# Gate and up products of a hybrid decoder layer: 512-column matmuls over the high and low part together, joins on VectorE, and a first weight sum accumulated by DMA

## The chip, the cores and the metric

The kernel runs on one core of one Trainium2 chip. The metric is device time in microseconds for one execution. The kernel before takes 619.7 us (median of 3 runs, 619.35 to 620.3). The engines spoken of are PE (TensorE matmuls; PEld is its weight load), DVE (VectorE), ACT (ScalarE), POOL (GpSimd, which here mostly issues DMAs) and SP (SyncE, which issues the plain loads). Each engine works off its own queue strictly in the order in which the program emits instructions.

## The reference

One decoder layer on 512 tokens of width 1024: an input projection, retention and sparse attention heads, an output projection with layer norm, and then the part that is changed here, the gated FFN:

```python
x = layer_norm(DEEPNORM_ALPHA * x + mix, ln_mix_gain, ln_mix_bias)
gate, up = jnp.split(x @ w_gate_up, 2, axis=-1)      # 1024 -> 2 x 2816
ffn = (jax.nn.silu(gate) * up) @ w_down              # 2816 -> 1024
return layer_norm(DEEPNORM_ALPHA * x + ffn, ln_ffn_gain, ln_ffn_bias)
```

## The kernel before

All is fp32. PE multiplies in a rounded form (`fp32r`), so every operand is split into a high part (rounded) and a low part (the rest), and a product is three matmuls: high by high, low by high, high by low. The helper `split` (L85 to L91) makes the parts: ACT copies the source into the rounded type (L86); the low part is either a subtraction on DVE (L91), or, when its engine is `None`, a negated copy on ACT (L88) to which a DMA issued by POOL adds the source (L89).

The FFN's first product is staged in 22 *cycles* (`g_cycle(n)`, L883, n = 0 to 21), one for each 128 hidden columns of gate and up. Tokens are cut into two halves of 256, the inner dimension into two halves of 512, and gate and up are the two halves of the columns; a scheme of Winograd's kind forms the 2 x 2 block product with seven block products in place of eight. The block operands of x are made ahead (`parts["11"]`, `["12"]`, `["22"]` and four sums `["s1"]` to `["s4"]`, each 128 x 2 (high, low) x 4 x 256). Those of the weights come from one raw load of 1 MB (`graw[n]`, gate `g` and up `u`; three buffers, loaded by SP) and four sums on DVE (`g_sum`, L824): `gs0` to `gs3`. In the text the four pieces that `g_conv` splits are called **A** (two 512-column halves, `gs1` and `gs0`), **B** (gate, raw), **C** (`gs2` and `gs3`) and **D** (one half, up, raw). A, B and C take their buffers `wh` and `wl` from a ring of four, and so does D.

In cycle n PE runs seven *steps* (`g_mm`, L849, 12 matmuls of 256 columns each), here named by their weight piece, with a prime where they belong to n + 1:

A0 into bank `ga(n)`; A1 into `gc(n)`; B0' into `ga(n+1)`; C0 into `ga(n)`; B1' into `gb(n+1)`; C1 into `ga(n)`; D into `gc(n)`.

Banks are read between the steps that add to them: ACT copies `ga` after A0 (`t2`, L894), after C0 (`t7`, L916) and after B0' (`t1`, L863); DVE adds `gc` to `t7` (L925) before D adds to `gc`; DVE adds `gb` (L867), ACT applies Silu to it (L871), and ACT applies Silu to the second token half straight from `ga` after C1 (L952). `g_end` (L877) adds `gc` to `t2` and multiplies both halves in the next cycle. So C0 may not start before ACT has read `ga` for t2, C1 not before it has read it for t7, and D not before DVE has read `gc`. The hidden units land in `hu`, six tiles of four slots; the sixth is in memory slot `s9`.

Beside step C1 and D, the cycle makes the weights of the next: B of n + 2, the sums of n + 2, C and D of n + 1; A of n + 1 is made in the middle of cycle n. The raw load of n + 4 is issued at the end of cycle n and waits until raw buffer n + 1 is no longer read. `FIRST = 4` is the first cycle whose B steps run inside another cycle. In cycle 21 nothing is left to make for gate and up, and `prepare_down` (L1247) converts the first weights and hidden units of the down projection in its place (`conv_w`, `conv_h`).

Of the kernel before, what the change touches and what calls it, by code (L numbers as in the profile page):

```python
# [53 lines left out]
def hybrid_layer_kernel(ctx: ExitStack, tc: tile.TileContext, xT, x, pos, w0, wf, wt, wo,  # L54
# [760 lines left out]

    def g_sum(n, eng=V, which=slice(0, 4)):
        if n >= NF:
            return
# [4 lines left out]
        for dst, a, b in ((0, u[:, :S], g[:, :S]), (1, u[:, S:], t[0]), (2, u[:, S:], u[:, :S]), (3, g[:, S:], t[1]))[which]:
            eng.tensor_tensor(t[dst], a, b, op=ALU.subtract)  # L824
# [23 lines left out]

    def g_mm(n, acc, kind, i, q, first):  # L849
        h, l = gw[n, kind]  # L850
        steps = [(k, a, b) for k in range(4) for a, b in ((h, 0), (l, 0), (h, 1))]
        if n == 0:
            steps.sort(key=lambda x: x[2])
        for j, (k, a, b) in enumerate(steps):
            T.matmul(gp[n][acc], lhsT=a[:, i * S + k * P:i * S + k * P + P], rhs=parts[q][:, b, k],  # L855
                     start=first and j == 0, stop=j == 11, skip_group_check=True)
# [4 lines left out]

    def g_t1(n):
        A.copy(gp[n]["h1"], gp[n]["a"])  # L863

    def g_add1(n):
        h1 = gp[n]["h1"]
        V.tensor_tensor(h1, h1, gp[n]["b"], op=ALU.add)  # L867
# [9 lines left out]
    def g_end(n):  # L877
        g = gp[n]
        V.tensor_tensor(g["t2"], g["t2"], g["c"], op=ALU.add)
        V.tensor_tensor(g["h1"], g["h1"], g["t2"], op=ALU.mult)  # L880
        V.tensor_tensor(g["h2"], g["h2"], g["t7"], op=ALU.mult)

    def g_cycle(n, between=None):  # L883
# [10 lines left out]
        A.copy(gp[n]["t2"], gp[n]["a"])  # L894
# [16 lines left out]
        c = gp[n]["c"]  # L911
        if n == NF - 1:
            c = tmp("gc")[:, :Q]
            A.copy(c, gp[n]["c"])
# [596 lines left out]
```

## Time and profile before

| what | before |
|---|---|
| median of 3 runs | 619.7 us |
| the profiled execution | 619.74 us |
| its span in the profile | 617.9 us |
| of the span: gate and up, from the first `ga` to the first `dl` matmul | 273.4 to 498.2 us |
| ACT, share of the span busy | 52% |
| DMA bytes | 97.97 MB |

The profiled execution's span lies 1.8 us below its own time; the rest is outside what the profile records. Engine times in a timeline are a start and a length; matmuls overlap, so their pace is read from start to start. "idle before" says what an engine waited for.

### The profile page before, as it was taken

How to read it: one execution, taken by the hardware profiler on the slowest of the kernel's cores; microseconds unless marked ns; L12 is line 12 of the kernel's file. 1: busy time of each engine (PE TensorE's matmuls, PEld its weight loads, DVE VectorE, ACT ScalarE, POOL GpSimd, SP SyncE). 2: the span in 40 equal slices, each digit the busy share in tenths (PEclk: the TensorE clock that was granted, in tenths of full speed). 3: DMA queues.
4: the chain of work that ended last, by engine and by line, in shares of the span. 5: the costliest groups of instructions: out<-in, count | busy, mean ns of one | idle time of the engine just before them, and what ended most of it. 6: DMA issues, size and time to landing. Idle time of an engine off the chain costs nothing.

```text
span 617.9 us, 9846 instructions
## 1 busy us (share of the span) xinstructions
PE 608.2 (98%) x3732; PEld 545.6 (88%) x3732; DVE 512.8 (83%) x953; ACT 323.0 (52%) x576; POOL 114.0 (18%) x118
## 2 busy tenths in 40 slices
PE   9999999999999999999999999999999999999994
PEld 7988888888888878889999999999999988888884
DVE  6897687898879877979998989898888888977856
ACT  5643444334343765777754555555455685648300
POOL 1176232421455000242000000000000021214010
PEclk9999999999999999999999999999999999999998
DMA  9887444778533962596333232332323379589602
GB/s 307 290 227 207 132 112 126 185 177 218 136 103 102 322 266 94 134 232 131 91 132 137 74 133 85 121 100 106 118 88 124 102 192 221 157 226 300 195 35 102
DMA packets 31584, 97.97 MB, mean 159 GB/s; under 512 B 3328, under 2 KB 9024, under 8 KB 25904
## 3 DMA queue, kind: packets, MB, share of 16 engines
q1 hardware_dynamic: 20464, 76.23, 35.9%
q0 software_dynamic: 10336, 19.86, 17.9%
q10 hardware_dynamic: 736, 1.25, 0.6%
q8 instruction: 29, 0.48, 0.3%
q14 instruction: 19, 0.16, 0.1%
HBM read 74.52 MB, written 2.10 MB: 124 GB/s over the span
## 4 chain that ended last, share of the span: by engine, by line
PE 82%; DVE 6%; issue 5%; DMA 3%; POOL 2%; ACT 1%; POOLq 0%; DVEq 0%; ACTq 0%
PE ga L855 19%; PE gc L855 10%; PE pf L95 5%; PE pf L94 5%; PE pf L96 5%; PE gb L855 4%; PE acc L205 4%; PE dl L95 2%; PE dl L96 2%; PE dl L94 2%; PE pt L94 2%; PE pt L96 2%; PE pt L95 2%; PE dr L96 2%; PE dr L95 2%
## 5 line engine op out<-in xcount | busy, mean ns | idle before, releaser
L86 ACT CAST wh<-raw 128x1024 fp32r<-128x1024 f32 x43 | 45.0, 1050 | 50.9 <-issue 20.6
L89 POOL DMA_DIRECT2D slot<-hu x9 | 10.9, 1337 | 235.0 <-ACT slot L88 233.8
L94 PE MATMUL pf<-xh,wh 128*128 128x512 f32 x128 | 50.0, 391 | 0.0
L95 PE MATMUL pf<-xl,wh 128*128 128x512 f32 x128 | 50.0, 390 | 0.0
L96 PE MATMUL pf<-xh,wl 128*128 128x512 f32 x128 | 49.9, 390 | 0.0
L91 DVE TENSOR_TENSOR wl<-raw,wh 128x1024 fp32r<-128x1024 f32 x24 | 29.1, 1224 | 14.2 <-ACT wh L86 14.2
L94 PE MATMUL pt<-wh,xh 128*128 128x512 f32 x96 | 39.1, 408 | 0.0
L96 PE MATMUL pt<-wh,xl 128*128 128x512 f32 x96 | 37.6, 391 | 0.0
L95 PE MATMUL pt<-wl,xh 128*128 128x512 f32 x96 | 37.5, 390 | 0.0
L824 DVE TENSOR_TENSOR gs<-graw,gs 128x512 f32<-128x512 f32 x44 | 30.3, 689 | 0.8
L440 POOL TENSOR_TENSOR rs<-ve,half 128x1 f32<-128x1 f32 (+1 forms) x11 | 11.8, 1069 | 102.6 <-DVE ve L439 102.4
L824 DVE TENSOR_TENSOR gs<-graw 128x512 f32<-128x512 f32 x44 | 30.2, 685 | 0.0
L96 PEld LDWEIGHTS pf<-xh,wl 128*128 128x128 f32 x128 | 24.0, 188 | 5.1
L94 PEld LDWEIGHTS pf<-xh,wh 128*128 128x128 f32 x128 | 24.0, 188 | 4.6
L95 PEld LDWEIGHTS pf<-xl,wh 128*128 128x128 f32 x128 | 24.1, 188 | 4.5
L89 POOL DMA_DIRECT2D wl<-raw x19 | 16.9, 891 | 59.2 <-ACT wl L88 52.3
L402 DVE MAX8 m<-score 128x8 f32<-128x256 f32 (+2 forms) x48 | 26.8, 558 | 1.1
L403 DVE MATCH_REPLACE8 score<-m,score 128x256 f32<-128x256 f32 (+2 forms) x48 | 26.0, 543 | 0.0
L385 ACT ACTIVATE lg<-lg 128x256 f32<-128x256 f32 (+2 forms) x24 | 10.9, 474 | 24.6 <-PE lg L384 22.6
L96 PEld LDWEIGHTS pt<-wh,xl 128*128 128x128 f32 x96 | 18.0, 188 | 3.9
L95 PEld LDWEIGHTS pt<-wl,xh 128*128 128x128 f32 x96 | 18.1, 189 | 3.1
L94 PEld LDWEIGHTS pt<-wh,xh 128*128 128x128 f32 x96 | 18.1, 188 | 3.1
(1123 smaller groups left out, 2076.3 us busy)
## 6 DMA issues: line engine op xcount, KB each, us to landing
graw<-in_wgu_dram SPq DMA_DIRECT2D x22, 1024.0 KB, 4.8
wl<-raw POOLq DMA_DIRECT2D x19, 512.0 KB, 5.6
raw<-in_wf_dram SPq DMA_DIRECT2D x8, 1024.0 KB, 7.4
raw<-in_wo_dram SPq DMA_DIRECT2D x8, 1024.0 KB, 4.8
raw<-in_wt_dram SPq DMA_DIRECT2D x6, 1024.0 KB, 5.5
r<-in_wd_dram SPq DMA_DIRECT2D x12, 512.0 KB, 5.6
draw<-in_wd_dram SPq DMA_DIRECT2D x8, 512.0 KB, 5.8
w0s<-in_w_dram SPq DMA_DIRECT2D x8, 320.0 KB, 4.8
```

Source lines behind the costliest of these rows:

```text
L86: A.copy(hi, src)
L89: nc.gpsimd.dma_start(lo.bitcast(F32), src, accum_op=ALU.add)
L91: eng_lo.tensor_tensor(lo, src, hi.bitcast(F32), op=ALU.subtract)
L94: T.matmul(acc, lhsT=lh, rhs=rh, start=first, stop=False, **kw)
L95: T.matmul(acc, lhsT=lh, rhs=rl, start=False, stop=False, **kw)
L96: T.matmul(acc, lhsT=ll, rhs=rh, start=False, stop=last, **kw)
L205: T.matmul(acc0[i][:, o:], lhsT=a[:, i * P:i * P + P], rhs=b[kt][:, o:], start=(kt == 0 and p == 0), stop=(kt == KT - 1 and p == 2))
L402: V.max(m8, a)
L403: V.match_replace(out=a, in_to_replace=m8, in_values=a, imm_value=TAKEN)
L440: G.tensor_tensor(r[:, :n], e[:, :n], half[:, :n], op=ALU.pow)
L824: eng.tensor_tensor(t[dst], a, b, op=ALU.subtract)
L855: T.matmul(gp[n][acc], lhsT=a[:, i * S + k * P:i * S + k * P + P], rhs=parts[q][:, b, k], start=first and j == 0, stop=j == 11, skip_group ...
```

## The change

From n = 4 on (`wide(n)`), three things are different; cycles 0 to 3 keep their form.

* A step is 8 matmuls. Four have 512 columns: the high weights against the high and the low part of x side by side, into a whole bank, whose first half then holds high by high and whose second half high by low. Four have 256 columns: the low weights against the high part, into the first half. The two halves of a bank are added on DVE (`g_join`) after the copy or the sum has been made 512 wide.
* Sum `gs0` is made in its own place in memory slot `s9` (`firsts`): SP loads half of up there ahead (`g_ahead`), and POOL issues a DMA that adds half of gate straight from memory (`g_plus1`). Sum `gs2` is made in the raw buffer by a DMA of the same kind (`g_plus3`). Signs are turned so that the sums are additions; the minus goes to the copies `t2` and `t7` (`g_minus`) and to the subtractions after them. DVE is left with two of the four sums. The first combinations of x (`combine`) are written with another operation for the same reason.
* The low part of D always goes by ACT and an adding DMA, up to n = 14 into a tile of its own in `s10` (`lasts`). The order within a cycle is another: for n + 1 below 15, A is made ahead of t2 and B and D ahead of t7; from there on (`late`), A stands behind t2, B behind the join of t7, and D at the cycle's end.

```diff
     def g_sum(n, eng=V, which=slice(0, 4)):
...
+        if n >= FIRST:
+            t = gsum[n] = [firsts(n), tmp(f"gs{n}_1"), u[:, :S], tmp(f"gs{n}_3")]
+            eng.tensor_tensor(t[1], u[:, S:], t[0], op=ALU.add)
+            eng.tensor_tensor(t[3], g[:, S:], t[1], op=ALU.add)
+            return
...
+    def g_ahead(n):
+        if FIRST <= n < NF:
+            dma(firsts(n), wgu[order[n], :, 1, :S])
+    def g_plus1(n):
+        if FIRST <= n < NF:
+            nc.gpsimd.dma_start(firsts(n), wgu[order[n], :, 0, :S], accum_op=ALU.add)
+    def g_plus3(n):
+        if FIRST <= n < NF:
+            u = graw[n][:, 1]
+            nc.gpsimd.dma_start(u[:, :S], u[:, S:], accum_op=ALU.add)
...
     def g_conv(n, kind, eng=V, into=None):
...
+        if kind == "D" and wide(n):
+            eng = None
...
     def g_mm(n, acc, kind, i, q, first):
         h, l = gw[n, kind]
+        if wide(n):
+            ws = [slice(i * S + k * P, i * S + k * P + P) for k in range(4)]
+            for k in range(4):
+                T.matmul(two(gp[n][acc]), lhsT=h[:, ws[k]], rhs=parts[q][:, :, k], start=first and k == 0, stop=False,
+                         skip_group_check=True)
+            for k in range(4):
+                T.matmul(gp[n][acc][:, :Q], lhsT=l[:, ws[k]], rhs=parts[q][:, 0, k], start=False, stop=k == 3,
+                         skip_group_check=True)
+            return
...
+    def g_join(t):
+        V.tensor_tensor(t[:, :Q], t[:, :Q], t[:, Q:], op=ALU.add)
...
     def g_cycle(n, between=None):
...
+        if wide(n) and not late:
+            g_conv(n + 1, "A")
...
+        g_minus(n, "t2", "a")
...
+        if n == 0 or wide(n) and late:
+            g_conv(n + 1, "A")
...
+        if wide(n):
+            g_sum(n + 2)
+            if not late:
+                g_conv(n + 2, "B")
         g_mm(n, "a", "C", 0, "s3", False)
...
+        if wide(n):
+            if not late:
+                g_conv(n + 1, "D")
+                g_plus1(n + 4)
+            g_seven(n)()
+            g_join(gp[n]["t7"])
+            if between:
+                next(between)
+            if late:
+                g_conv(n + 2, "B")
+            g_mm(n, "a", "C", 1, "22", False)
+            if nxt:
+                g_add1(nxt)
+            g_conv(n + 1, "C")
+            if nxt:
+                g_silu1(nxt)
+            if n < NF - 1:
+                g_mm(n, "c", "D", 0, "s4", False)
+            A.copy(gp[n]["h2"], gp[n]["a"][:, Q:])
+            V.tensor_tensor(gp[n]["h2"], gp[n]["h2"], gp[n]["a"][:, :Q], op=ALU.add)
+            A.activation(gp[n]["h2"], gp[n]["h2"], AF.Silu)
+            if late:
+                g_conv(n + 1, "D")
+                g_plus1(n + 4)
+            g_plus3(n + 3)
+            g_load(n + 4)
+            g_ahead(n + 5)
+            return
```

First place: ACT around the end of cycle 3, before the change. `gh4C` and `gh5A` are the high parts of C of 4 and A of 5, `hu` Silu results, `gt` is t2 of 4.

```order
L871 ACTIVATE hu_3103<-hu_3103 128x256
L86 CAST gh4C<-gs_2_3048 128x512
L86 CAST gh4C<-gs_3_3049 128x512
L952 ACTIVATE hu_2584<-ga_2727 128x256
L86 CAST gh4D<-graw_2857 128x512
L894 COPY gt_3232<-ga_3104 128x256
L86 CAST gh5A<-gs_1_3172 128x512
```

The same place of the changed kernel; `lasts` is D of 4, its high part and then its negated low part.

```order
L921 ACTIVATE hu_3109<-hu_3109 128x256
L86 CAST gh4C<-graw_2857 128x512
L86 CAST gh4C<-gs_3_3054 128x512
L1049 ACTIVATE hu_2584<-ga_2727 128x256
L86 CAST lasts<-graw_2857 128x512
L88 ACTIVATE lasts<-graw_2857 128x512
L86 CAST gh5A<-gs_1_3170 128x512
L86 CAST gh5A<-firsts 128x512
L936 ACTIVATE gt_3228<-ga_3110 128x512
```

The low part of D and both halves of A now stand ahead of t2.

Second place: ACT of the changed kernel from the end of cycle 15 into cycle 16, which is late (`hu_3974` in the first two rows is the second token half of 15, `gl16D` the negated low part of D of 16, `gt` t2, `gu` t7, `hu_4401` in the last row t1).

```order
L1005 COPY hu_3974<-ga_4293 128x256
L1007 ACTIVATE hu_3974<-hu_3974 128x256
L86 CAST gh16D<-graw_4154 128x512
L88 ACTIVATE gl16D<-graw_4154 128x512
L936 ACTIVATE gt_4501<-ga_4402 128x512
L86 CAST gh17A<-gs_1_4412 128x512
L86 CAST gh17A<-firsts 128x512
L908 COPY hu_4401<-ga_4510 128x512
```

There, before, the Silu came straight from `ga` (no copy and no sum on DVE ahead of it), D had one row, and t2 and A followed in this same order.

Third place: ACT from cycle 20 into cycle 21, before; `dh(0, 0)` and `h_0` are the first converted weights and hidden units of the down projection, the last row is t2 of 21.

```order
L952 ACTIVATE hu_5191<-ga_5192 128x256
L86 CAST gh21D<-graw_5025 128x512
L86 CAST dh(0, 0)_5419<-draw_0_5284 128x1024
L86 CAST h_0_5423<-hu_2584 128x1024
L894 COPY gt_5440<-ga_5323 128x256
```

And of the changed kernel, where `firsts` in the first two rows is the second token half of 20.

```order
L1005 COPY firsts<-ga_4829 128x256
L1007 ACTIVATE firsts<-firsts 128x256
L86 CAST gh21D<-graw_4693 128x512
L88 ACTIVATE gl21D<-graw_4693 128x512
L86 CAST dh(0, 0)_5013<-draw_0_4902 128x1024
L86 CAST h_0_5017<-hu_2584 128x1024
L936 ACTIVATE gt_5030<-ga_4935 128x512
```

Two rows were put ahead of t2 of 21: the Silu's own copy and the negated low part of D; between copy and Silu stands a sum on DVE.

More of the change, by code (lines that the diff above doesn't have):

```diff
@@ L798, in hybrid_layer_kernel @@
                            })
-    hu = {}
+    hu, keep = {}, {}
     Q = 2 * P
@@ L805, in hT, with wide @@
         if i not in hu:
-            hu[i] = unit(("X0", "X1", "s8", "s2", "s10", "s9")[i], f"hu{i}")
+            hu[i] = keep["t1"] if i == 5 else unit(("X0", "X1", "s8", "s2", "s10")[i], f"hu{i}")
         return hu[i][:, f % 4]
     graw, gp = {}, {}
+    def wide(n):
+        return n >= FIRST
     def g_load(n):
@@ L814, in g_load, with firsts @@
             dma(graw[n], wgu[order[n]])
+    def firsts(n):
+        if "t1" not in keep:
+            keep["t1"] = unit("s9", "firsts")
+        return keep["t1"][:, (n + 2) % 4]
+    def g_ahead(n):
[8 more added lines that the diff above has]
+            nc.gpsimd.dma_start(u[:, :S], u[:, S:], accum_op=ALU.add)
     def g_sum(n, eng=V, which=slice(0, 4)):
@@ L835, in g_conv @@
         if kind == "D" and n == 1:
-            both = big.tile([P, 2, S], F32R, tag="s9", name="dheld")
+            both = big.tile([P, 2, S], F32R, tag="s10", name="dheld")
             h, l = both[:, 0], both[:, 1]
+        elif kind == "D" and FIRST <= n < 15:
+            if "d" not in keep:
+                keep["d"] = unit("s10", "lasts", F32R)
+            h, l = (keep["d"][:, 2 * (n % 2) + i] for i in range(2))
         elif into:
@@ L854, in g_mm @@
         for j, (k, a, b) in enumerate(steps):
[L855 removed]
+            T.matmul(gp[n][acc][:, :Q], lhsT=a[:, i * S + k * P:i * S + k * P + P], rhs=parts[q][:, b, k],
                      start=first and j == 0, stop=j == 11, skip_group_check=True)
@@ L889, in g_cycle @@
             next(between)
-        gp[n]["c"] = psu(f"gc{n}")[:, :Q]
-        g_mm(n, "c", "A", 1, "s1", True)
-        t = tmp(f"gt{n}")
-        gp[n]["t2"], gp[n]["t7"] = t[:, :Q], t[:, Q:]
-        A.copy(gp[n]["t2"], gp[n]["a"])
+        late = n + 1 >= 15
+        if wide(n) and not late:
+            g_conv(n + 1, "A")
+        w = S if wide(n) else Q
+        gp[n]["c"] = psu(f"gc{n}")[:, :w]
+        g_mm(n, "c", "A", 1, "s1", True)
+        if wide(n):
+            gp[n]["t2"], gp[n]["t7"] = tmp(f"gt{n}"), tmp(f"gu{n}")
+        else:
+            t = tmp(f"gt{n}")
+            gp[n]["t2"], gp[n]["t7"] = t[:, :Q], t[:, Q:]
+        g_minus(n, "t2", "a")
         if n == 1:
@@ L910, in g_cycle @@
             g_mm(3, "b", "B", 1, "12", True)
[L911 to L914, printed above, removed]
-            g_mm(n, "c", "D", 0, "s4", False)
-        A.copy(gp[n]["t7"], gp[n]["a"])
+        if wide(n):
+            if not late:
[14 more added lines that the diff above has]
+            if n < NF - 1:
+                g_mm(n, "c", "D", 0, "s4", False)
+            A.copy(gp[n]["h2"], gp[n]["a"][:, Q:])
[8 more added lines that the diff above has]
+            return
+        less = g_seven(n)
         if n == 0:
@@ L924, in g_cycle @@
             g_sum(2, V, slice(2, 4))
-        V.tensor_tensor(gp[n]["t7"], gp[n]["t7"], c, op=ALU.add)
+        less()
         if n in (2, 3):
             g_conv(n + 1, "A")
-        if between:
-            next(between)
         if n == 2:
@@ L949, in g_cycle @@
             g_sum(2, V, slice(0, 2))
-        if n < NF - 1 and not held(n):
+        if not held(n):
             g_mm(n, "c", "D", 0, "s4", False)
```

47 lines of the change are left out of this document (36 added, 11 removed).

## The prediction

> **What bounds the kernel now.** I read the page first, then one cycle of gate and up, engine by engine.
>
> ```profile
> PE 608.2 (98%) x3732; PEld 545.6 (88%) x3732; DVE 512.8 (83%) x953; ACT 323.0 (52%) x576; POOL 114.0 (18%) x118
> PE 82%; DVE 6%; issue 5%; DMA 3%; POOL 2%; ACT 1%; POOLq 0%; DVEq 0%; ACTq 0%
> ...
> 400.00:410.08 10.08, 10.08 (x86) 10.08 (x85) 8.65 (x17) 5.54 (x13) 0.00 (x0) 1.00 0.28 104
> ```
>
> The chain that ends last is 82% PE, and in one cycle (the window) PE is busy without a gap at full clock (1.00), DVE for 8.65 of 10.08 us. A busy PE isn't yet PE at its pace, so I look at starts.
>
> ```profile
> 400.25 0.28 PE L855 MATMUL ga<-parts,gh12A 128*128 128x256 f32 x1
> ...
> 410.33 0.28 PE L855 MATMUL ga<-parts,gh13A 128*128 128x256 f32 x1
> ...
> 541.71 0.39 PE L94 MATMUL dx<-dhp,slot 128*128 128x512 f32 x1
> ...
> 545.11 0.39 PE L94 MATMUL dx<-dhp,slot 128*128 128x512 f32 x1
> ```
>
> A cycle is 84 matmuls in 10.08 us: 0.120 us for 256 columns. The last two rows, of the down projection, are 15 matmuls apart: 0.2267 us for 512. Twice the columns cost 0.1067 us more, so 0.0133 us of each matmul doesn't depend on its columns. PE waits for nobody here: it is the bound, and what it saves is time, as long as ACT and DVE keep up.
>
> **What the change takes from PE.** A wide step is 4 x 0.2267 + 4 x 0.120 = 1.387 us in place of 12 x 0.120 = 1.440. Seven steps for n = 4 to 21 are 126 steps and 504 matmuls fewer: 504 x 0.0133 = **6.7 us**; a cycle becomes 9.71 us. That the operand comes in two blocks of 256 the trace doesn't show; between 0.2267 and 2 x 0.120 I take the first, since the array streams as many columns.
>
> The Trainium skill ("TensorE: Matmul & The Clock Gate", section "Back-to-back issue gap") puts the warm gap at N / 2.4 + 2.5 ns. By it 28 matmuls fewer in 18 cycles would give 1.3 us (an estimate from that page), not 6.7. The rows above disagree with its 2.5 ns: they show 13.3.
>
> **DVE.** Its costs from start to start, and ACT's:
>
> ```profile
> 404.15 0.41 DVE L879 TENSOR_TENSOR gt<-gt,gc 128x256 f32<-128x256 f32 x1
> 404.59 0.42 DVE L880 TENSOR_TENSOR hu<-hu,gt 128x256 f32<-128x256 f32 x1
> 404.94 0.42 DVE L881 TENSOR_TENSOR hu<-hu,gt 128x256 f32<-128x256 f32 x1
> 405.27 1.29 DVE L91 TENSOR_TENSOR gl13A<-gs,gh13A 128x512 fp32r<-128x512 f32 x2
> ...
> 408.34 1.29 DVE L91 TENSOR_TENSOR gl14B<-graw,gh14B 128x512 fp32r<-128x512 f32 x2 [1.31 <-ACT gh14B L86]
> ...
> 409.88 0.69 DVE L824 TENSOR_TENSOR gs<-graw 128x512 f32<-128x512 f32 x1
> 410.61 0.69 DVE L824 TENSOR_TENSOR gs<-graw,gs 128x512 f32<-128x512 f32 x1
> 411.22 0.68 DVE L824 TENSOR_TENSOR gs<-graw 128x512 f32<-128x512 f32 x1
> ```
>
> A 512-wide operation takes 0.73 if the next needs its result (409.88 to 410.61), else 0.60; a 256-wide one 0.44 or 0.33. Of a wide cycle go two sums and D's subtraction; t2, t7 and the gate sum become 512 wide; three joins and the sum for the second half come. What is left: 4 x 0.73 + 7 x 0.60 + 0.44 + 5 x 0.33 = **9.2 us** of 9.71. It fits, with 0.5 to spare where there were 1.31 idle.
>
> **ACT** gets three copies 0.22 us longer, the low part of D (0.53) and a copy beside the Silu (0.33): 5.54 + 1.5 = 7.1 us of 9.71. Load is no matter, but it works in order, and C0 and C1 on PE now wait for its t2 and t7 wherever these stand behind other work.
>
> ```profile
> 404.57 0.28 PE L855 MATMUL ga<-parts,gh12C 128*128 128x256 f32 x1
> ...
> 404.77 0.37 ACT L863 COPY hu<-ga 128x256 f32<-128x256 f32 x1 [0.25 <-PE ga L855]
> ...
> 319.45 0.42 DVE L867 TENSOR_TENSOR hu<-hu,gb 128x256 f32<-128x256 f32 x1
> ...
> 319.90 0.42 ACT L871 ACTIVATE hu<-hu 128x256 f32<-128x256 f32 x1 [1.78 <-DVE hu L867]
> 320.22 1.12 ACT L86 CAST gh4C<-gs 128x512 fp32r<-128x512 f32 x2
> 321.25 0.38 ACT L952 ACTIVATE hu<-ga 128x256 f32<-128x256 f32 x1
> 321.52 0.61 ACT L86 CAST gh4D<-graw 128x512 fp32r<-128x512 f32 x1
> 322.04 0.37 ACT L894 COPY gt<-ga 128x256 f32<-128x256 f32 x1
> ...
> 323.93 0.28 PE L855 MATMUL ga<-parts,gh4C 128*128 128x256 f32 x1
> ...
> 294.92 0.61 ACT L86 CAST dheld<-graw 128x512 fp32r<-128x512 f32 x1
> 295.43 0.63 ACT L88 ACTIVATE dheld<-graw 128x512 fp32r<-128x512 f32 x1
> 295.96 0.36 ACT L894 COPY gt<-ga 128x256 f32<-128x256 f32 x1
> ...
> L692 ACT COPY kept<-tr 128x512 f32<-128x512 f32 x4 | 2.3, 586 | 0.7 <-PE tr L674 0.7
> ```
>
> On ACT a copy starts 0.20 after the step before it has ended on PE (404.57 to 404.77). A 512-wide piece is 0.52 (two of C in 1.03), D's negated low part 0.53, a 256-wide Silu of a half in SBUF 0.33, a 512-wide copy from PSUM 0.59 long (L692) and about 0.49 to the next start.
>
> *Cycle 4, the first wide one.* DVE reaches the gate sum of 4 at 318.8 in place of 319.45: two sums of 4 less are 1.2 us, and half of that is lost to waits, for t7 of 3 and for B's buffer, which comes free only after B1' of 4. The sum is now 0.73 and its join 0.44, so ACT starts the Silu at 320.0. Then, as ordered now: C until 321.4, second half 321.6, D and its low part 322.7, both halves of A 323.7, t2 read by 324.3. C0 could start at 323.7 (323.93, less 0.11 for two wide steps before the cycle and two in it): PE stands 0.65 us. t7 comes late too, behind B, t1 and D: 0.25 us more before C1. **-0.9 us.** From cycle 5 to 13 the same order has slack: t7 is read about 0.4 us before C1 needs it.
>
> *Late cycles.* Call x the start of DVE's sum for the second half. ACT then runs Silu (x + 0.46), D (0.33 later), its low part (0.52), t2 (0.53), A (0.49): the first half of A is done at x + 2.93. DVE takes A 1.2, two sums 1.33, t7 0.73, join 0.33, B 1.2, gate sum 0.73, join 0.33, C 1.2, and is at the next x: a **loop of 10.0 us** against PE's 9.71. Before, the Silu came from `ga` and D's low part was DVE's, so there was no such loop. In cycle 14, the first late one, B stands behind t7: C0 ends 5.55 into the cycle, ACT has copied by 6.35, and t7, join, B, gate sum, join and C on DVE put x at 10.9, 1.2 into cycle 15. Each cycle adds 0.3; C0 waits for t2 (x + 2.47, against 4.16) once x lies 1.7 in, from cycle 17 to 20: 0.15 + 3 x 0.3. **-1.1 us.**
>
> *Cycle 21.* ACT's chain to t2, before:
>
> ```profile
> 490.37 0.61 ACT L86 CAST gh21D<-graw 128x512 fp32r<-128x512 f32 x1
> 491.21 1.05 ACT L86 CAST dh(0, 0)_5419<-draw 128x1024 fp32r<-128x1024 f32 x1 [0.23 <-ACT gh21D L86]
> 492.16 1.05 ACT L86 CAST h<-hu 128x1024 fp32r<-128x1024 f32 x1
> 493.11 0.36 ACT L894 COPY gt<-ga 128x256 f32<-128x256 f32 x1
> ...
> 493.85 0.28 PE L855 MATMUL ga<-parts,gh21C 128*128 128x256 f32 x1
> ```
>
> t2 ended 0.4 us before C0, which has no B' in front of it in this cycle. Now x falls about at the cycle's start; Silu 0.46 to 0.78, D 1.3, low part 1.8, weights 2.8, hidden units 3.7, t2 read by 4.35; C0 is due at 2.77. **-1.6 us.** The second pair of down operands is then ready about as PE asks for it.
>
> **DMA, POOL and SP.** Three adding DMAs a cycle (256 KB each) and one load ahead are new.
>
> ```profile
> 296.00:300.00 4.00, 4.00 (x36) 4.00 (x35) 3.28 (x6) 3.00 (x9) 0.88 (x1) 1.00 0.38 66
> 520.00:560.00 40.00, 40.00 (x178) 33.15 (x177) 32.47 (x43) 21.61 (x33) 6.89 (x7) 1.00 0.82 216
> ...
> graw<-in_wgu_dram SPq DMA_DIRECT2D x22, 1024.0 KB, 4.8
> wl<-raw POOLq DMA_DIRECT2D x19, 512.0 KB, 5.6
> slot<-hu POOLq DMA_DIRECT2D x9, 256.0 KB, 6.9
> parts<-cs POOLq DMA_DIRECT2D x1, 256.0 KB, 7.7
> dheld<-graw POOLq DMA_DIRECT2D x1, 256.0 KB, 3.3
> ```
>
> One alone takes 0.38 x 4 = 1.5 us of the 16 queues and lands in 3.3. A cycle is then 0.28 x 10.08 = 2.8 for the load, 0.7 for the quarter ahead, 4.6 for three: 8.1 of 9.71, 84%, as in 520 to 560, where PE stands nowhere. POOL issues three in about 2.7 us (0.88 each) and waits in order: D's for ACT, then the add to `firsts` for its load, then the one in the raw buffer. Their readers come one to two cycles later. SP's load waits for D's add and the quarter behind it for the load; both have about a cycle. Tight is D in the late cycles: its low part lands L after ACT's write at x + 1.93, and PE wants it at about 9.5 into the cycle: L below 5.6 with x at 2.0. I take 5 (between 3.3 alone and the rows in bursts), and 0.3 us in cycle 21, where it is wanted at 6.65.
>
> The turned signs, the other operation in `combine` and cycles 1 to 3 cost nothing: same widths, and PE covers them.
>
> **Sum.** -6.7 + 0.9 + 1.1 + 1.6 + 0.4 (D of 21, and 0.1 at the second pair) = -2.7. From the profiled execution's 619.74 (the median is 619.7) that is **617.0 us**.
>
> **Rivals.**
>
> *Handoffs hide.* If ACT's and DVE's hand-overs are quicker than my rows, or a lag doesn't build up, only about 0.9 us is lost: 613.9. For it: PE never stands now. Against: the orders above. 17%.
>
> *PE gains little.* If the second block costs a fixed part as a matmul does, 512 columns take 0.24, a cycle stays 10.08, the late loop (10.0) hides, and cycles 4 and 21 still cost about 2: 621.7. Against: the 0.2267 rows. 6%. The gap that the Trainium skill gives ("TensorE: Matmul & The Clock Gate", section "Back-to-back issue gap") would end beside it: the same stalls with 1.3 us taken, 620.4, an estimate.
>
> *D lands late (slower).* Place: cycles 15 to 21. Price: with L = 7.9 (near the `parts` row) the cycle is 10.5 us, 0.8 x 6 over 9.71, and in cycle 21 D's second four matmuls start 9.7 in, so that its end lies 4.6 late: -6.7 + 0.9 + 4.9 + 4.6 + 0.1, so 623.5. At L = 7 it breaks even: it decides above that. For: 6.9 and 7.7 in the rows. Against: those stand in bursts behind others, while D's is the first of its three. 15%.
>
> *DVE pays more.* With 0.05 us for each new wait (seven a cycle), DVE fills 9.6 of 9.71 and the late loop is 10.3: 1.5 us more, 618.5 to 619. 12%.
>
> **How the numbers follow.** Forecast 50%, 615 to 618.5 by the terms' own doubt (half of each stall either way). Two in ten may fall outside: below 613.5 lies little, above 620.5 D landing late and a part of the little gain. Range 613.5 to 620.5. Faster by over 0.2% (below 618.5; about what a measurement can tell from no change): forecast, hidden handoffs and part of the DVE case, 71%. Within: 13%. Slower: 16%.
>
> **What would show it.** 512-column steps of 1.387 us on PE and 9.71 us a cycle from 5 to 13 (wrong if the matmuls start 0.24 apart); a PE gap before C0 of 4 and C0 of 21 behind t2, about 0.65 and 1.6 us; late cycles of 10.0 us from 17 on, their wait on t2 by ACT; DVE busy about 94% in cycles 5 to 13; D's adds landing in about 5 us. If PE waits for D's low part or DVE for a DMA, the DMA rival holds.

## The result, and the profile after

| | median us | range us | ratio to before, 95% interval |
|---|---|---|---|
| before, beside the first runs | 619.66 | 619.35 to 620.3 | 1 |
| changed, first runs | 625.0 | 624.77 to 626.23 | 1.0095 [1.0081, 1.0109] |
| changed, second set (`e0_again`) | 621.66 | 620.06 to 624.36 | 1.0032 [1.0018, 1.0047] |
| changed, third set (`e8_unchanged_again`) | 624.17 | 620.1 to 626.47 | 1.0072 [1.0049, 1.0095] |

The change makes the kernel slower by 0.3 to 1%; forecast were 617.0 us and a range of 613.5 to 620.5. One execution of the first runs took 3458 us, was disturbed and is left out (counted in, the median is 625.62); since it was the profiled one, the profile after is here that of `e0_again`, whose profiled execution took 624.36 us (span 622.3). That is the slowest of its ten, so what its profile shows as lost is more than the median lost.

The page (busy time of the engines, then the chain that ends last) and the window of one cycle, the one of n = 12, with the columns PE, PEld, DVE, ACT, POOL, granted clock, DMA share, GB/s:

```profile
PE 606.9 (98%) x3228; PEld 520.2 (84%) x3228; DVE 523.7 (84%) x971; ACT 348.3 (56%) x612; POOL 161.0 (26%) x172
PE 73%; DMA 9%; DVE 9%; issue 4%; ACT 4%; POOL 1%; POOLq 0%; DVEq 0%; SPq 0%; ACTq 0%
...
403.61:413.43 9.82, 9.82 (x59) 8.58 (x57) 9.16 (x18) 7.03 (x14) 2.60 (x3) 1.00 0.86 199
```

The chain is the first sign: PE fell from 82% to 73% and DMA rose from 3% to 9%. The undisturbed cycle is 9.82 us, where 9.71 were forecast; DVE is busy for 9.16 (forecast 9.2), ACT for 7.03 (7.1), and the DMA engines for 86% (84%). So the engines' loads were sized right, and the matmuls were not quite. Their starts:

```profile
403.61 1.09 PE L889 MATMUL ga<-parts,gh12A 128*128 128x512 f32 x4
404.54 0.63 PE L892 MATMUL ga<-parts,gl12A 128*128 128x256 f32 x4
```

Four of 512 columns take 0.93 us from start to start, not 4 x 0.2267 = 0.907. With 0.47 for the other four a step is 1.403.

Where the rest went is seen in the lengths of the cycles, from the start of A0 to the next A0 on PE (for 21, five steps long, to the first matmul of the down projection):

| cycle | before | `e0_again` | `e8_unchanged_again` |
|---|---|---|---|
| 4 | 10.08 | 10.73 | 10.72 |
| 5 | 10.08 | 10.02 | 10.04 |
| 7 | 10.08 | 10.50 | 9.97 |
| 9 | 10.08 | 14.05 | 10.74 |
| 10 | 10.08 | 10.04 | 9.82 |
| 13 | 10.08 | 9.82 | 15.20 |
| 14 | 10.08 | 9.82 | 10.16 |
| 18 | 10.08 | 10.95 | 9.82 |
| 19, 20 | 10.08 | 10.46, 9.99 | 9.98, 9.99 |
| 21 | 7.20 | 8.60 | 8.59 |
| all others | 10.08 | 9.80 to 9.83 | 9.82 to 9.83 |

Cycles 4 and 21 are long in both, as forecast. But 6.9 and 7.0 us over the pace go into cycles that differ from one execution to the next: mostly 7, 9 and 18 in the first, 9 and 13 in the second, and no term of the forecast speaks of them. What is waited for in `e0_again` between 315 and 505 us (total, times, longest) is led by:

```profile
POOL firsts L830 <- DMA firsts<-in_wgu_dram: 85.2, 15, 10.9
...
DVE gs L843 <- DMA graw<-in_wgu_dram: 5.4, 3, 3.1
...
ACT gh11B L86 <- DMA graw<-in_wgu_dram: 4.1, 1, 4.1
```

GpSimd stands 85 us at the add to `firsts`, which waits for the load ahead. DVE and ACT wait for a *raw load*. The chain of work back from the long wait in cycle 9 (start, length, what) joins the two:

```profile
346.47 8.70 DMA firsts<-in_wgu_dram
...
355.75 0.52 POOL firsts L830
356.27 0.52 POOL graw L835
356.79 9.60 DMA lasts<-graw
...
366.51 9.69 DMA graw<-in_wgu_dram
...
376.83 0.61 ACT gh11B L86
```

The load ahead lands at 355.2 and releases GpSimd, which issues its add, the add in the raw buffer, and only then, at 356.79, the add for D's low part. That lands 9.6 us later and releases the raw buffer; SP issues the raw load at 366.51, it lands at 376.2, and ACT makes B. PE has by then run out of work:

```profile
376.21 0.63 PE L892 MATMUL gb<-part,gl10B 128*128 128x256 f32 x4
379.52 1.20 PE L889 MATMUL ga<-part,gh9C 128*128 128x512 f32 x4 [2.67 <-ACT gu L936]
```

Behind that raw load stands, on SP, the next load ahead (issued at 366.88), and GpSimd waits for that one before it may issue D's next add but one:

```profile
356.79 1.56 POOL L89 DMA_DIRECT2D lasts<-graw  x1
...
366.22 0.86 POOL L89 DMA_DIRECT2D lasts<-graw  x1 [0.56 <-ACT lasts L88]
377.99 0.86 POOL L830 DMA_DIRECT2D firsts<-in_wgu_dram  x1 [10.91 <-DMA firsts<-in_wgu_dram]
...
379.27 1.35 POOL L89 DMA_DIRECT2D lasts<-graw  x1
```

This is a **loop of two queues**: D's add of n lands, SP issues the raw load of n + 3 and behind it the load ahead of n + 4, that lands, and GpSimd issues its add and then D's add of n + 2. It spans two cycles, 19.6 us, and holds two landings; here it took 22.5 (356.79 to 379.27). The raw load hangs on it with a landing of its own.

The wait isn't all. The granted clock (last but two) in the stretches behind it:

```profile
379.50:381.00 1.50, 1.48 (x8) 1.31 (x9) 1.47 (x3) 0.99 (x2) 1.12 (x2) 0.94 1.05 404
381.00:382.50 1.50, 1.50 (x6) 1.21 (x6) 1.47 (x4) 0.68 (x2) 0.00 (x0) 0.50 0.81 232
382.50:384.00 1.50, 1.50 (x7) 1.40 (x6) 0.76 (x3) 0.73 (x2) 0.00 (x0) 0.50 0.99 176
384.00:390.00 6.00, 6.00 (x34) 5.20 (x34) 5.55 (x10) 4.09 (x9) 1.75 (x2) 0.98 1.15 211
```

After the gap PE ran at half clock for some 3 us, so cycle 9 lost 2.8 by the wait and 1.4 by the clock. In `e8_unchanged_again` it was the same in cycle 13: a gap of 2.74 us, then 0.50 from 421.5 to 426.0, 2.9 lost by the wait and 2.5 by the clock.

The account for this execution, from A0 of 4 to the first down matmul, 183.74 us against 178.56: matmuls 17 x (9.825 - 10.08) - 0.18 = -4.5; cycle 4 +0.9; cycle 21 +1.6; late cycles 19 and 20 about +0.3; cycles 5, 7, 9, 10, 18 and the rest of 19 +6.9. That is +5.2, as measured. Everything ahead of it is 0.8 shorter and what follows equal; that part varies too (in `e8_unchanged_again` what lies ahead is 0.7 longer than before).

### The profile page after: what moved, and what is told of

The parts are those of the page before. It is cut to its first block, busy times and chain, and to the rows that moved or that the text cites. A ratio compares the mean times of both kernels' runs of the same rounds, so it can differ in the third digit from the quotient of the medians.

```text
span 3456.3 us, 9062 instructions
## 1 busy us (share of the span) xinstructions
PE 3447.5 (100%) x3228; PEld 2620.5 (76%) x3228; DVE 532.0 (15%) x971; ACT 360.3 (10%) x612; POOL 160.4 (5%) x172
## 4 chain that ended last, share of the span: by engine, by line
PE 100%; DVE 0%; DVEq 0%; issue 0%
PE ga L889 11%; PE ga L892 6%; PE gc L889 6%; PE pf L95 5%; PE pf L96 5%; PE pf L94 5%; PE pt L96 4%; PE ga L899 4%; PE acc L205 4%; PE pt L94 4%; PE pt L95 4%; PE gb L889 3%; PE gc L892 3%; PE mx L96 2%; PE dl L94 2%; PE mx L95 2%
## 5 line engine op out<-in xcount | busy, mean ns | idle before, releaser
L96 PE MATMUL pf<-xh,wl 128*128 128x512 f32 x128 | 217.2, 1696 | 0.0
L94 PE MATMUL pf<-xh,wh 128*128 128x512 f32 x128 | 217.1, 1696 | 0.0
L95 PE MATMUL pf<-xl,wh 128*128 128x512 f32 x128 | 216.8, 1694 | 0.0
L94 PE MATMUL pt<-wh,xh 128*128 128x512 f32 x96 | 170.5, 1776 | 0.0
L96 PE MATMUL pt<-wh,xl 128*128 128x512 f32 x96 | 162.8, 1696 | 0.0
L95 PE MATMUL pt<-wl,xh 128*128 128x512 f32 x96 | 161.9, 1686 | 0.0
L96 PEld LDWEIGHTS pf<-xh,wl 128*128 128x128 f32 x128 | 117.1, 915 | 52.2 <-issue 52.2
L95 PEld LDWEIGHTS pf<-xl,wh 128*128 128x128 f32 x128 | 117.2, 915 | 48.4 <-issue 48.4
L94 PEld LDWEIGHTS pf<-xh,wh 128*128 128x128 f32 x128 | 116.1, 907 | 47.7 <-issue 47.7
L96 PE MATMUL dx<-dhp,slot 128*128 128x512 f32 x36 | 61.0, 1695 | 0.0
L94 PE MATMUL dx<-dhp,slot 128*128 128x512 f32 x36 | 61.0, 1695 | 0.0
```

Of the source, the lines that this page charges most:

```text
L94: T.matmul(acc, lhsT=lh, rhs=rh, start=first, stop=False, **kw)
L95: T.matmul(acc, lhsT=lh, rhs=rl, start=False, stop=False, **kw)
L96: T.matmul(acc, lhsT=ll, rhs=rh, start=False, stop=last, **kw)
```

## The experiments

Each is a version of the changed kernel, timed beside the kernel before.

**The changed kernel again.** No edit.

> The changed kernel unchanged, for an undisturbed trace (the profiled execution of the result ran PE some four times slower throughout, at 3458 us, and can't be read stage by stage). All theories: 625 us again. Theory P (the 512-column matmul in two blocks of 256 is not cheaper than two of 256): its starts lie 0.24 us apart and a cycle from 5 to 13 stays 10.08 us or more. Theory S (the matmuls are cheap but hand-overs stall PE): starts 0.227 apart, and PE gaps before C0, C1 or D in every cycle, 12 us in all. Theory D (the low part of D lands late): PE gaps in the middle of step D, in cycles 15 to 21 only.

Measured: 621.66 us, and the profile shown above. None of the three theories written down fits it: the starts lie 0.23 us apart, the gaps come in a few cycles only, and none is in the middle of step D. The profile gave the theory that the rest tests: the loop of two queues.

**The load ahead goes first** (`e1_ahead_first`, in both places where they stand).

```diff
-            g_load(n + 4)
             g_ahead(n + 5)
+            g_load(n + 4)
```

> In every cycle SP issues the load ahead of firsts before the raw load, in place of after it; nothing else. Theory Q (a loop through two queues: D's add waits on POOL behind the add to firsts, that waits for the load ahead, that stands on SP behind the raw load, and that waits for D's add of two cycles before): the load ahead lands before POOL comes to it, D's add is issued when ACT is done with it, the raw load starts some 3 us earlier in a cycle, PE's stalls of cycles 7, 9 and 18 to 20 go (about 6 us in the profile of the unchanged kernel), and the median falls from 621.7 by 2 to 5 us, to 617 to 619.5. Theory B (too many bytes: the 16 queues are 85% busy and everything lands late whatever its order): the same bytes, so the stalls stay and the time is within 1 us of 621.7.

Measured: 618.57 us (617.76 to 620.17), 0.9984 [0.9975, 0.9994], 3.1 under `e0_again`. Cycles 5 to 17 are 9.82 or 9.83 throughout, with 4 at 10.73, 19 and 20 at 10.01 and 21 at 8.60: what the forecast had named stays, what it hadn't is gone. (3.1 is against the lowest of the three medians of the changed kernel; against the others it is more.) GpSimd's 85 us at L830 are gone from the waits, and D's add, up to n = 14, waits for ACT alone:

```profile
POOL lasts L89 <- ACT lasts L88: 36.7, 10, 8.0
```

How the swap helps is seen on SP:

```profile
344.48 0.33 SPq L80 DMA_DIRECT2D graw<-in_wgu_dram  x1
344.91 0.64 SPq L80 DMA_DIRECT2D firsts<-in_wgu_dram  x1
```

A load ahead is still issued 0.43 us behind a raw load, but it is the raw load of a cycle earlier. So the loop isn't cut: it now has three cycles, 29.5 us, for its two landings. A second loop stays at two cycles: the add in the raw buffer (L835) waits on GpSimd for the raw load itself, ahead of D's next add but one. It has room here: the raw load of 354.57 lands at 361.87, L835 follows at 362.42, and D's add behind it still waits 2.8 us for ACT.

**Narrow matmuls again** (`e2_narrow_products`, on `e1_ahead_first`): each of 512 columns as two of 256.

```diff
-                T.matmul(two(gp[n][acc]), lhsT=h[:, ws[k]], rhs=parts[q][:, :, k], ...)
+                for b in range(2):
+                    T.matmul(gp[n][acc][:, b * Q:b * Q + Q], lhsT=h[:, ws[k]], rhs=parts[q][:, b, k], ...)
```

> As the run with the load ahead first, but each 512-column matmul is two of 256 again (84 matmuls a cycle, the two halves into the two halves of the bank); all else as there. Theory M (the matmuls do save time, 18 x (10.08 - 9.82) = 4.7 us by the step of 1.404 us seen in the unchanged kernel): slower than the run with the load ahead first by 3.5 to 5 us. Theory N (PE's own saving is worth nothing since ACT, DVE or DMA set the pace of the wide cycles): within 1 us of it.

Measured: 622.71 us (622.16 to 622.86), 1.0044 [1.0029, 1.0059]. The wide matmuls are worth 4.1 us in time, not 6.7. All cycles from 5 to 20 are 10.08 here, the late ones too.

**The load ahead twice** (`e3_ahead_twice`, on `e1_ahead_first`): the same 256 KB loaded two times.

```diff
-            dma(firsts(n), wgu[order[n], :, 1, :S])
+            for _ in range(2):
+                dma(firsts(n), wgu[order[n], :, 1, :S])
```

> As the run with the load ahead first, but the load ahead of firsts is issued twice, the same data to the same place: 256 KB more a cycle (some 0.7 us of the 16 queues, 84% to 91% of a cycle). Theory Q: bytes have room, within 1 us of the run with it once. Theory B: more bytes, so transfers land later still and PE stands again, 2 us or more slower.

Measured: 619.93 us (618.33 to 621.9), 1.0006 [0.9993, 1.0019]: 1.4 more than `e1_ahead_first`, between what the two theories expected. The DMA share from 310 to 420 us rose from 0.90 to 0.98. The edit is more than bytes, though: SP waits for the first copy to land before it issues the second (12 times from 315 to 430 us, 88.8 us in all), and GpSimd waits at L831 for the second (9 times, 15.3 us). So what the bytes alone cost isn't shown; with this wait added they cost half of what the order of two issues on SP does.

**Copies first** (`e4_copies_first`, on `e1_ahead_first`): in cycle 4, A of 5 goes behind t2; in cycle 21, the first down operands do.

```diff
-        if between:
-            next(between)
         late = n + 1 >= 15
-        if wide(n) and not late:
+        if wide(n) and not late and n > FIRST:
             g_conv(n + 1, "A")
...
         g_minus(n, "t2", "a")
+        if between:
+            next(between)
+        if n == FIRST:
+            g_conv(n + 1, "A")
```

> As the run with the load ahead first, and t2 is read ahead of other work on ACT in two cycles: in cycle 4 A of 5 stands behind t2, in cycle 21 the first down weights and hidden units do. Theory H (the prediction's: these orders cost 0.65 and 1.6 us of PE): PE's gap before C0 of 21 goes (1.5 us in the unchanged kernel), the one before C0 of 4 (0.58) goes, and it is faster than the run with the load ahead first by 1.5 to 2.2 us. Rival: the work put behind t2 is late itself (the first down operands), and no more than 0.7 us is left.

Measured: 617.34 us (616.85 to 619.04), 0.9963 [0.995, 0.9976]: 1.2 better than `e1_ahead_first`, under both kernels, and the fastest version of this study that leaves no product out. It is less than the 1.5 to 2.2 expected, since in cycle 4 the wait moved two steps on, from t2 to t7:

```profile
324.94 1.09 PE L889 MATMUL gb<-part,gh5B 128*128 128x512 f32 x4
325.87 0.63 PE L892 MATMUL gb<-part,gl5B 128*128 128x256 f32 x4
327.16 1.19 PE L889 MATMUL ga<-part,gh4C 128*128 128x512 f32 x4 [0.66 <-ACT gu L936]
```

B1' lasts 2.22 in place of 1.40, so cycle 4 is 10.74 as before the edit; cycle 21 fell from 8.60 to 7.68.

**One run of columns** (`e5_one_block`, on `e4_copies_first`). The product with the low part of x is replaced by another one, so this version leaves a needed product out.

```diff
-                ... rhs=parts[q][:, :, k], ...
+                ... rhs=parts[q][:, 0, min(k, 2):min(k, 2) + 2], ...
```

> Built on e4_copies_first (617.3). The 512-column matmuls read their moving operand as one run of 512 columns of the high part (pieces k and k+1) in place of two runs of 256 (high and low of piece k), so the product of the high weights with the low part of x is replaced by another one; instructions, weights, banks and waits stay. Theory S (the second run of columns costs about 6 ns a matmul, which is why a step is 1.404 and not 1.387 us): 504 x 0.0058 = 2.9 us less wherever PE sets the pace: 614.4 to 615.6, steps of 1.387 us or a little under. Rival (the 6 ns come from something else, as the change between 512 and 256 columns, the second bank half or the clock): within 0.6 of e4, steps of 1.404.

Measured: 617.21 us (616.26 to 618.1), and the same pace:

```profile
398.42 1.09 PE L889 MATMUL ga<-parts,gh12A 128*128 128x512 f32 x4
399.35 0.64 PE L892 MATMUL ga<-parts,gl12A 128*128 128x256 f32 x4
399.82 1.09 PE L889 MATMUL gc<-parts,gh12A 128*128 128x512 f32 x4
```

Still 0.93. The second run of columns costs nothing here; that theory falls.

**The add one cycle later** (`e6_add_later`, on the changed kernel, SP as there).

```diff
                 g_conv(n + 1, "D")
-                g_plus1(n + 4)
+            g_plus1(n + 3)
             g_seven(n)()
...
                 g_conv(n + 1, "D")
-                g_plus1(n + 4)
...
-            g_plus1(n + 4)
+            g_plus1(n + 3)
...
-            g_plus1(4)
```

> The changed kernel with its own order on SP (raw load, then the load ahead), and the add to firsts issued one cycle later on GpSimd. Theory Q (a loop of two queues: the add on GpSimd waits for a load ahead that stands on SP behind a raw load, which waits for the add of D that stands on GpSimd behind it): the loop is opened at its other queue, so the stalls in cycles 7, 9 and 18 go as they did in e1: 617.8 to 619.4. Rival O (e1 won because the quarter goes into the DMA rings ahead of the 1 MB, whatever waits on GpSimd): the order on SP is as it was, so nothing is won, 621 to 624. What could spoil it: the add now lands about a cycle before its reader, so that in late cycles DVE may wait for it.

Measured: 621.9 us (619.75 to 624.02), 1.004 [1.0025, 1.0055]: inside the rival's range. In the profiled execution, the fastest of them at 619.75, cycles 7, 9, 13 and 18 are without a stall, but what was said to be able to spoil it came: the add for 6 stood behind the add for D of 4, which waited for ACT until 322.23, in cycle 4,

```profile
322.23 0.86 POOL L89 DMA_DIRECT2D lasts<-graw  x1 [6.64 <-ACT lasts L88]
322.77 1.21 POOL L830 DMA_DIRECT2D firsts<-in_wgu_dram  x1
```

DVE waited 3.4 us for it and C1 took 4.11 us to the next step's start. By its median the run doesn't decide between the theories. (In the trace of `e1_ahead_first` the quarter still goes out right behind a load of 1 MB, at 344.91 and 344.48, so what the rival takes for its gain isn't seen there.)

**Two more copies ahead** (`e7_copies_two`, on `e4_copies_first`).

```diff
         if n == NF - 1:
-            c = tmp("gc")
-            A.copy(c, g["c"])
+            c = g["sc"]
...
-            if not late:
+            if not late and n > FIRST:
                 g_conv(n + 2, "B")
...
-            if late:
+            if late or n == FIRST:
                 g_conv(n + 2, "B")
...
         if between:
+            gc = tmp("gc")
+            A.copy(gc, gp[n]["c"])
+            gp[n]["sc"] = gc
             next(between)
```

> Built on e4_copies_first: in cycle 4 piece B of 6 goes behind the join of t7 (t7 is late by 0.8 us there in e4), and in cycle 21 ACT reads gc for t7 before it converts the first down operands (0.55 us between C0 and D in e4). Theory H (what is left over the pace of PE in gate and up is ACT's order in these two cycles): 0.7 + 0.4 less, 616.2 (615.8 to 616.8). Rival (the wait moves on to the next step or to the down projection): within 0.4 of e4, 617.0 to 617.7.

Measured: 618.71 us (618.07 to 620.6), 0.9989 [0.998, 0.9998], above the ranges of both. Cycle 4 is clean, but the wait stands one cycle later, with B of 7 late because its raw load is:

```profile
333.39 1.14 ACT L86 CAST gh7B<-graw 128x512 fp32r<-128x512 f32 x2 [0.90 <-DMA graw<-in_wgu_dram]
```

From A0 of 4 to the first down matmul its profile needs 176.0 us, as that of `e4_copies_first` does (175.9). It is what follows that takes 121.3 and not 119.7: the wait moved on into the down projection too, as the rival said, where PE waits for the second pair of operands.

```profile
497.58 0.50 PE L96 MATMUL dl<-dh(0, 1)_5054,h 128*128 128x512 f32 x1 [0.63 <-DVE h L91]
```

**The changed kernel, a third time.** No edit.

> The changed kernel once more, beside the others on one chip, since it took 625.6 in the first runs and 621.7 in e0_again. Theory Q (small differences in when DMAs land are made larger by the loop of two queues): anywhere from 620 to 626, with a spread of its own runs above 2 us, while e6 and e7 spread under 2. Rival (the first chip was slower in general): 621.7 within 0.5.

Measured: 624.17 us (620.1 to 626.47). The time of the first runs was no property of its chip: the unchanged kernel ranges over 6.4 us on one, where before ranges over 1.8 beside it. One part of the expectation failed: `e6_add_later` and `e7_copies_two` spread by 4.3 and 2.5 us, not by under 2. The longest cycle is 13 here, where DVE waited 3.2 us for the raw load of 15.

**D's low part on DVE** (`e9_low_d_dve`, on the changed kernel): no adding DMA for D up to 14.

```diff
-        if kind == "D" and wide(n):
+        if kind == "D" and n >= 15:
             eng = None
```

> The changed kernel with its own order on SP and GpSimd, but the low part of D up to 14 is a subtraction on DVE, as before the change, in place of ACT and an adding DMA. The raw load then waits for no DMA of GpSimd, so the loop of two queues (D's add of n, raw load of n + 3, load ahead of n + 4, its add, D's add of n + 2) is cut at a third place, while GpSimd goes on waiting for the load ahead. Theory Q: the stalls of cycles 7, 9, 13 and 18 go, DVE rises by 0.6 us to about 9.4 of 9.82 a cycle, and ACT has 0.5 us less ahead of t2 of 4: 617.4 to 619.2. Rival D (DVE is then too full, as the prediction's case 'DVE pays more' has it): the stalls come back as waits for t7 and for C, 620 to 623.

Measured: 619.83 us (618.11 to 621.38), 1.0004 [0.9992, 1.0015], between the two ranges. In the profiled execution (618.92) only the cycles 4 (11.14, with PE waiting 0.9 us for DVE's t7) and 21 are long, while GpSimd still waits, and DVE is full. A row of the waits, and the window from 320 to 420 us:

```profile
POOL firsts L830 <- DMA firsts<-in_wgu_dram: 97.4, 15, 9.9
```

```profile
320.00:420.00 100.00, 99.08 (x563) 86.36 (x562) 98.27 (x183) 65.60 (x134) 18.49 (x22) 1.00 0.74 189
```

GpSimd waits 97 us for the loads ahead, more than in `e0_again`, and nobody is late, since D's add no longer stands behind it: the wait in itself costs nothing, it harms by what is queued after it. (The DMA share fell with the adds that went, from 0.85 in `e0_again` to 0.74 here, so this run alone doesn't part the queue from the bytes; `e1_ahead_first`, with the same bytes, does.) With DVE at 98% the other executions have no slack, which may be why the median is 1 us higher than the profiled one.

**512 columns only** (`e10_all_wide`, on `e4_copies_first`): low by low is added.

```diff
-                T.matmul(gp[n][acc][:, :Q], lhsT=l[:, ws[k]], rhs=parts[q][:, 0, k], ...)
+                T.matmul(two(gp[n][acc]), lhsT=l[:, ws[k]], rhs=parts[q][:, :, k], ...)
```

> Built on e4_copies_first; the four 256-column matmuls of a wide step (low weights by the high part) become 512 columns over both parts, so low by low is added. A measurement of the 512-column matmul in this loop by itself: e5 has shown that the second run of columns isn't why four take 0.93 us and not 0.907. If the mixing of widths is why (a 512 next to a 256): eight in a row at 0.2267, a step of 1.81 us. If it is a property of this loop: 0.2325, a step of 1.86 us. The time itself is about 126 x 0.42 = 53 us more than e4 and says nothing.

Measured in one execution: 666.61 us, and

```profile
399.77 1.07 PE L889 MATMUL ga<-part,gh11B 128*128 128x512 f32 x4
400.68 1.07 PE L892 MATMUL ga<-part,gl11B 128*128 128x512 f32 x4
401.59 1.07 PE L889 MATMUL ga<-parts,gh10C 128*128 128x512 f32 x4
```

Eight take 1.82 us, 0.227 each, two runs of columns and all. What costs is the mixing of widths. The cost doesn't fall on one matmul: from start to start between 340 and 440 us, the four of 512 columns in `e4_copies_first` take 234, 235, 232 and 228 ns on average.

**The add later, mended** (`e11_add_later_b`, on `e6_add_later`): the adds for 4, 5 and 6 stand where the change has them.

```diff
-            g_plus1(n + 3)
+            if n < FIRST - 1:
+                g_plus1(n + 4)
             g_plus3(n + 3)
...
             g_ahead(4)
+            g_plus1(4)
```

> e6_add_later mended: from cycle 4 on the add to firsts is issued one cycle later and behind D's add, as in e6, but the adds for 4, 5 and 6 stand where the change has them, since in e6 the add for 6 stood behind D's wait in cycle 4 and cost PE 2.7 us. SP keeps the order of the changed kernel. Theory Q: the way from D's add to D's add takes three cycles (29.5 us) in place of two (19.6) for the same 18 to 19 us of landings, so the stalls of 7, 9, 13 and 18 go and the runs spread by less than 2 us: 617.8 to 619.4. Rival O (e1 won by the order of the quarter and the 1 MB in the DMA rings): 620.5 to 623, with a spread above 3.

Measured: 619.1 us (617.68 to 620.26), 0.9995 [0.9985, 1.0006]. The median is in the range of the loop theory and under the rival's; the spread of 2.6 lies between what the two said. SP's order is that of the changed kernel, so the order of the transfers isn't what `e1_ahead_first` won by: given a third cycle at either queue, the loop lets go. In its profile cycles 6 to 17 are 9.81 to 9.83; 5 (10.51) and 19 (10.44) are still long; in 5 DVE waits 1.8 us for the later add.

**Fewer changes of width** (`e12_turned`, on `e4_copies_first`): in A0, C0 and C1 the 256-column matmuls come first.

```diff
+            turn = not first and kind != "D"
+            for low in ((1, 0) if turn else (0, 1)):
+                for k in range(4):
...
```

> Built on e4_copies_first; in the steps A0, C0 and C1 the four 256-column matmuls come ahead of the four 512-column ones, so that widths change 8 times a cycle and not 14. e10 gave 0.2265 us for 512 columns among their like, and a step of four and four takes 1.403 and not 1.387. Theory W (16 ns are paid for each change there and back, whichever of the two costs it): 3 x 16 = 0.05 us less a cycle, 9.77 and not 9.82, 18 x 0.05 = 0.9 us: 616.4 (616.0 to 616.9). Rival (what costs is another thing, as four 512s at the start of a group in a bank; or the low weights, asked for first, now come late): cycles of 9.82 or more, 617.3 to 618.5.

Measured: 617.7 us (616.31 to 618.44), 0.9968 [0.9956, 0.998], and on PE:

```profile
398.61 0.64 PE L893 MATMUL ga<-parts,gl12A 128*128 128x256 f32 x4
399.09 1.09 PE L896 MATMUL ga<-parts,gh12A 128*128 128x512 f32 x4
400.02 1.07 PE L896 MATMUL gc<-parts,gh12A 128*128 128x512 f32 x4
400.93 0.64 PE L893 MATMUL gc<-parts,gl12A 128*128 128x256 f32 x4
...
408.38 0.64 PE L893 MATMUL ga<-parts,gl13A 128*128 128x256 f32 x4
```

Four of 512 behind a 256 take 0.93, four behind a 512 take 0.91. The cycle is 9.77, as expected. The time didn't follow: 617.7 against 617.34 with overlapping ranges, in the rival's range for the time though not for the cycle. The profile explains it in part. From A0 of 4 to the first down matmul it is only 0.5 us shorter than that of `e4_copies_first` (175.4 and 175.9), for the late cycles stay at the 10.0 us of their loop:

```profile
470.02 1.09 PE L896 MATMUL ga<-part,gh20B 128*128 128x512 f32 x4
...
480.01 1.09 PE L896 MATMUL ga<-part,gh21B 128*128 128x512 f32 x4
```

They are 9.98 to 10.00 here, from 18 to 20. And what follows takes 120.8 us, not 119.7, with a wait in the down projection, far from the edit:

```profile
564.36 0.50 PE L96 MATMUL dl<-dhp,slot 128*128 128x512 f32 x1 [0.70 <-DMA slot<-hu]
```

**Both orders** (`e13_both_orders`): `e4_copies_first` with the add later, as in `e11_add_later_b`.

> Built on e4_copies_first (load ahead issued before the raw load on SP); in addition the add to firsts is issued behind D's add one cycle later from cycle 4 on, as in e11. Theory Q (what is left of the spread and of the small stalls in the profiles of e1 and e4 is still the loop of two queues): a spread of its runs below 1.5 us, median 616.6 to 617.4. Rival (the loop is fully opened by either order and what is left is bytes and ACT's order): as e4, 617.0 to 618, spread 2 or more.

Measured: 618.52 us (617.02 to 619.46), 0.998 [0.997, 0.9989], 1.2 above `e4_copies_first`, and a spread of 2.4. The loop is not what is left of the spread; the kernel before, beside it, spread by 1.8. In its profile cycle 5 takes 10.88: issued a cycle later, the add to `firsts` now lands after DVE wants it.

```profile
DVE gs L843 <- DMA firsts<-in_wgu_dram: 5.7, 10, 2.1
```

The longest of these waits, 2.1 us, is the one for the sums of 7 in cycle 5. So the later add costs something of its own, which `e4_copies_first` doesn't pay.

## Why the prediction was wrong, by its own steps

* **The failed step is the paragraph on DMA, POOL and SP**: "SP's load waits for D's add and the quarter behind it for the load; both have about a cycle". In the sum it stands at nothing. It lists each wait with its own slack, but doesn't join them: GpSimd's wait for the quarter stands ahead of D's add, and so the waits close into one loop, which has two cycles, 19.6 us, for two landings. With 9.6 for D's add, 11.1 from the issue of the load ahead to GpSimd's add (366.88 to 377.99) and the issues between, it took 22.5. The landings were taken too short as well: 5 us for D's add, which in `e0_again` landed after 8.8 (median of the eleven for n = 4 to 14, the longest 11.0), while the raw loads went from 4.8 before to 7.1. At 5 and 4.8 the loop would close in some 12 us (an estimate from these numbers) and fit into its two cycles with room. Its stalls cost 6.9 us in the `e0_again` profile, half clock included; giving the loop a third cycle at SP (`e1_ahead_first`, -3.1 in the medians) or at GpSimd (`e11_add_later_b`, -2.6) takes most of what the median carries, with the same bytes.
* **The rival on the other side had the engine right and the place wrong.** It put a late D into cycles 15 to 21, by PE waiting for the low part. There D's adds landed fast, 3.3 to 3.7 us but for one of 5.3, and PE never waited for one. What was late was the raw load behind D's adds, mostly in cycles 5 to 14. The test the forecast gave, "DVE for a DMA", did come true. That the rival's 623.5 lies near the measured times is chance: its two terms, late cycles of 10.5 us and 4.6 us in cycle 21, didn't occur.
* **Matmuls: right mechanism, size too large.** -6.7 said, -4.5 in the profile, 4.1 by `e2_narrow_products`. Among its like a 512 is 0.2267 as taken; four of them behind a 256 cost some 22 ns more together, and the 256s behind them 6 ns less, which makes 126 times 16 ns or 2 us. The rival that the second block costs a fixed part falls with `e5_one_block`. As for the Trainium skill's gap ("TensorE: Matmul & The Clock Gate", section "Back-to-back issue gap"), the 0.227 of `e10_all_wide` for 512 columns is again 13 ns over 512 / 2.4 and not its 2.5. That section of the Trainium skill gives the formula for a matmul by itself; the 131 ns that it gives for a stream of 512-column matmuls lies further off.
* **Cycle 4: right.** 0.9 lost was said, 10.73 - 9.825 = 0.9 measured, behind t2, as said:

```profile
322.54 0.63 PE L892 MATMUL ga<-part,gl5B 128*128 128x256 f32 x4
323.59 1.19 PE L889 MATMUL ga<-parts,gh4C 128*128 128x512 f32 x4 [0.41 <-ACT gt L936]
```

* **Cycle 21: right for t2, with 0.4 too much.** 1.6 lost was said, and 0.4 for D and the second pair; measured 8.60 - 7.02 = 1.6. The 0.4 didn't come: D's add for 21 landed in 3.3 us, where 5 were taken. (With cycles 4 and 21 the rival that hand-overs hide falls.) C0 starts by ACT's t2 of 497.6, behind the rows that were named:

```profile
495.18 0.63 ACT L88 ACTIVATE gl21D<-graw 128x512 fp32r<-128x512 f32 x1
495.72 1.04 ACT L86 CAST dh(0, 0)_5013<-draw 128x1024 fp32r<-128x1024 f32 x1
496.66 1.04 ACT L86 CAST h<-hu 128x1024 fp32r<-128x1024 f32 x1
497.60 0.59 ACT L936 ACTIVATE gt<-ga 128x512 f32<-128x512 f32 x1
```

* **Late cycles: the loop of 10.0 us is there** (10.01 in `e1_ahead_first`, 10.00 in `e12_turned`), but from 18 or 19 on. Against 9.82 it costs 0.4, not 1.1: a mis-sized term, in part because PE was slower than taken.
* DVE and ACT as computed; "DVE pays more" didn't occur until `e9_low_d_dve` filled it.

With the loop out of the way, the forecast's own terms as measured, -4.5 + 0.9 + 0.4 + 1.6, give -1.6; `e1_ahead_first` is -1.0. In its profile gate and up, from A0 of 4, are 1.7 shorter than before, as these terms say, and what follows is 0.4 longer.

What stays open: why executions still differ by 2 us and more when the loop has room. The profiles of the versions show where they differ: A0 of 4 starts at 318.7 to 320.3 us, cycle 5 takes 9.8 to 10.9, and what follows gate and up 119.7 to 121.3. Whether the medians of `e7_copies_two` and `e13_both_orders` lie above `e4_copies_first` for the reasons that their one profile each shows isn't tested. Nor is it shown why 512s among 256s take longer.

## What to carry to other kernels

Where a change adds waits to two in-order queues, write down for each waiting instruction what stands behind it, and follow this until it ends or comes back: a loop's time is the sum of its landings under load, to be held against the cycles that it spans, and no single slack shows it. Take the landings from a stretch that is as loaded as the new kernel will be. An issue that others wait for goes ahead of one that may wait long; here the swap of two lines on SP gave the loop a cycle more and was worth 3.1 us, three quarters of what the wide matmuls bring. Runs that spread from 620 to 626 us where the old kernel's spread by 2 were, here, the sign that the kernel hung on landing times.

## What the hardware showed that was not expected

* A 512-column matmul costs 0.227 us among its like; a run of four behind one of 256 costs some 20 ns more in all (0.93 against 0.91), spread over the four.
* After the 2.67 us gap of cycle 9 the granted clock was 0.50 from 381.0 to 384.0, and after one of 2.74 us in `e8_unchanged_again` from 421.5 to 426.0. In `e6_add_later` a gap of 2.4 us cost no clock (1.00 behind it):

```profile
330.50:332.00 1.50, 1.32 (x7) 1.16 (x8) 1.43 (x4) 0.00 (x0) 0.00 (x0) 1.00 0.80 208
```

  The Trainium skill ("TensorE: Matmul & The Clock Gate", section "Part 1: The HAM clock gate") ties the half clock to an idle window of about 3.4 us that runs freely. The factor of one half agrees; here a gap shorter than that was enough.
* In `e0_again` D's adds of 256 KB landed in 3.3 to 5.3 us for n = 15 to 21, and after 8.8 (median) for n = 4 to 14, where they stand among other transfers; the longest took 11.0.
